# Sixteen broadcast loads of a state-space scan issued by GpSimd instead of SyncE

## The chip, the core and the metric

The kernel runs on one core of one Trainium2 chip. The metric is the device time of one execution in microseconds (us); lower is better. Three executions of the kernel before took 815.21, 816.28 and 816.71 us, so its median is 816.28 us. A core has five instruction streams that run side by side and wait for each other through semaphores: PE (TensorE, matrix products; PEld is its weight load), DVE (VectorE), ACT (ScalarE), POOL (GpSimd) and SP (SyncE, which here issues DMAs and does nothing else). Each stream takes its instructions strictly in order. Sixteen DMA engines move the data of every DMA, whichever stream issued it.

## The reference

The program is one decoder block on 16 meta tokens and 512 real ones: an input projection, a Mamba-2 mixer (SSD) and an S5 mixer side by side, an output projection and an MLP. The part that the change touches is the inside of the SSD mixer. Cut to that part:

```python
a_cs = jnp.cumsum(dtc * a, axis=2)
seg = a_cs[:, :, :, None] - a_cs[:, :, None, :]
decay = jnp.exp(jnp.where(causal, seg, -jnp.inf))
cb = jnp.einsum('bclgn,bcsgn->bclsg', cc, bc)
y_diag = jnp.einsum('bclsg,bclsgr,bcsgrp->bclgrp', cb, decay, xdt)
y_off = jnp.einsum('bclgn,bcgrpn,bclgr->bclgrp', cc, prev, jnp.exp(a_cs))
y = (y_diag + y_off + xc * d)
```

`a_cs` is one running sum for each of 16 heads along the tokens. The kernel needs it, and its exponential, spread over partitions: a row of 128 tokens of one head has to stand in all 128 partitions (`decay`), and a row of `exp(a_cs)` in the 64 partitions of its head (`y_off`).

## The kernel before

The work goes by stages that overlap. First come the input projection's columns for S5 (`u`), for the SSD inputs (`pxb`) and for the gate (`pz`), with the eight blocks of the S5 scan (`s5_block`) between them; then the S5 mixer's gated projection with `w_glu` (`pv`, `pg`, line 891 on); then the output projection with `w_out` (`acc`) and the MLP in four quarters. Nearly every matrix product is done three times, because float32 operands are split into a high and a low part: ACT writes `whi`, and DVE (`wlo`, line 118) or an adding DMA from POOL (line 122) writes the low part. The weights come in through three buffers of one kind (`raw`, line 105): SP loads 512 KB into one, in 1024 rows of 512 bytes for `w_in` and `w_glu`, and can load into it again when the low part of the weights that stood there has been written.

The SSD scan is the loop over `ch` at line 735. It runs over the 16 meta tokens (chunk 0) and four chunks of 128 tokens, with a state `S` of 16 heads that each chunk updates. It is placed by a scheduler between the matrix products of the gated projection, which runs at the same time. The scheduler sets the order of each engine's instructions when the program is built, so an engine meets both kinds of work in one fixed order.

For each of chunks 1 to 4:

- `erep` (line 766) gets `exp(a_cs)`: two loads, each to 64 partitions, of 8 rows of 512 bytes per partition. That is 256 KB and 512 rows in one load. There is one buffer, so the load waits until DVE has multiplied with the chunk before (`yt`, line 796).
- `ab` (line 771) gets `a_cs`, for 8 heads at a time: two loads, for `g` = 0 and 1, each to 128 partitions of 8 rows of 512 bytes. That is 512 KB and 1024 rows in one load. There are two buffers, so each load waits until the products of the chunk before that used this buffer (`pyd`, line 789) are done.
- POOL then puts the causal mask on `ab` (`affine_select`, line 773), ACT takes the exponential of the 8 heads (line 777), DVE multiplies it by `cb` (line 779), and PE uses it as the moving operand of `pyd`.
- PE also makes `pyo` from the state (line 793), DVE adds the parts up (lines 796 to 803), ACT squares the result (line 805), DVE adds the squares up in `sqs`, and PE sums those over the partitions into `pq1` (line 813).

`aD` and `eD`, which hold `a_cs` and its exponential in DRAM, were written long before (lines 671 and 672).

The S5 blocks before this stage have a chain of small DMAs of their own: a block's `lag` goes to DRAM (`Kd`, line 539), comes back shifted in four loads as `Tp` (line 541), and is the weight of the block's `py` products (line 594). Block 7 is the last one.

Of the kernel before, what the change touches and what calls it, by code (L numbers as in the profile page):

```python
# [18 lines left out]
P = 128  # L19
# [26 lines left out]
def bc(ap, axis, n):  # L46
    a = ap.unsqueeze(axis)
    shape = list(a.shape)
    shape[axis] = n
    return a.broadcast_to(shape)  # L50
# [3 lines left out]
def hybrid_block_kernel(ctx, tc, x, meta_tokens, g_mix, w_in, conv_w, conv_b, dt_bias, a_log, d_ssd,  # L54
                        g_ssd, lam_re, lam_im, log_step, b_re, b_im, c_re, c_im, d_s5, w_glu, b_glu,
                        g_s5, w_out, g_mlp, w_up, w_down, g_final, out, dbg=None):
    nc = tc.nc
    V, A, G, T = nc.vector, nc.scalar, nc.gpsimd, nc.tensor
    dma = nc.sync.dma_start
    dma2 = nc.sync.dma_start  # L60
# [18 lines left out]
    def bank(name, dt=F32):  # L79
        tag = KIND.get(name, "x")  # L80
        return ps.tile([P, 512], dt, tag=tag, name=name, bufs=TAGS[tag])
# [16 lines left out]
    def vadd(out, in0, in1):  # L98
        V.tensor_tensor(out=out, in0=in0, in1=in1, op=ALU.add)  # L99
# [367 lines left out]
    def col(nm, i):  # L467
        c = row[nm] + i
        return pcol[:, c:c + 1]
# [199 lines left out]
    aD = dr.tile([NH, SEQ], F32, name="aD")  # L669
# [61 lines left out]
    erep = sd.tile([P, KD, P], F32, tag="erep", name="erep", bufs=1)  # L731
# [3 lines left out]
    for ch in range(NCH):  # L735
        n = NM if ch == 0 else P
        t0 = 0 if ch == 0 else NM + (ch - 1) * P
        tk = slice(t0, t0 + n)

        pcb = bank("pcb")  # L740
        if ch > 0:
            for g in range(2):
                T.matmul(pcb[:, g * P:(g + 1) * P], lhsT=bcT[:, g, tk], rhs=bcT[:, 2 + g, tk])
        if ch < 4:
            btok = sd.tile([P, 2, P], F32, tag="btok", name="btok", bufs=1)
            for g in range(2, 4):
                T.transpose(pcb[0:n, g * P:(g + 1) * P], bcT[:, g - 2, tk], ident)
            A.copy(btok[0:n], pcb[0:n, 2 * P:4 * P].rearrange("p (g q) -> p g q", g=2))
        if ch > 0:
            xdt = sd.tile([P, NH, 64], F32, tag="xdt", name="xdt", bufs=1)  # L750
            xde = sd.tile([P, NH, 64], F32, tag="xde", name="xde", bufs=1)
        for h in range(2):
            ptx = bank("ptx")
            for k in range(4):
                T.transpose(ptx[0:n, k * P:(k + 1) * P], xc[:, 4 * h + k, tk], ident)
            pv = ptx[0:n].rearrange("p (h d) -> p h d", d=64)
            hs = slice(8 * h, 8 * h + 8)
            if ch > 0:
                V.tensor_tensor(out=xdt[0:n, hs], in0=pv, in1=bc(dt[0:n, ch, hs], 2, 64), op=ALU.mult)
            if ch < 4:  # L760
                V.tensor_tensor(out=xde[0:n, hs], in0=pv, in1=bc(wdt[0:n, ch, hs], 2, 64), op=ALU.mult)
        if ch > 0:
            lt = slice((ch - 1) * P, ch * P)
            if ch > 1:
                erep = sd.tile([P, KD, P], F32, tag="erep", name="erep", bufs=1)
            for q in range(2):
                dma2(out=erep[64 * q:64 * q + 64],
                     in_=eD.rearrange("(r q) l -> q r l", q=2)[q, :, lt].partition_broadcast(64))
            Gm = []
            for g in range(2):  # L770
                ab = sd.tile([P, 8, P], F32, tag="ab", name="ab", bufs=2)
                dma2(out=ab, in_=aD[8 * g:8 * g + 8, lt].partition_broadcast(P))
                G.affine_select(out=ab, in_=ab, pattern=[[0, 8], [1, P]], compare_op=ALU.is_ge, fill=-1e30, base=0,
                                channel_multiplier=-1)
                with tc.issue_after(last_silu.ins):
                    for h in range(8):
                        A.activation(out=ab[:, h], in_=ab[:, h], func=AF.Exp,
                                     bias=neg_a[:, ch, 8 * g + h:8 * g + h + 1])
                V.tensor_tensor(out=ab, in0=ab, in1=bc(pcb[:, g * P:(g + 1) * P], 1, 8), op=ALU.mult)
                Gm.append(ab)  # L780
            for h in range(2):
                pyd = bank("pyd")
                pyo = bank("pyo")
                for r in range(4):
                    pr = 4 * h + r
                    o = slice(r * P, (r + 1) * P)
                    for q in range(2):
                        hd = 2 * pr + q
                        T.matmul(pyd[64 * q:64 * q + 64, o], lhsT=xdt[:, hd], rhs=Gm[h][:, hd % 8])
                for r in range(4):  # L790
                    pr = 4 * h + r
                    o = slice(r * P, (r + 1) * P)
                    T.matmul(pyo[:, o], lhsT=S[0][:, 2 * pr:2 * pr + 2].rearrange("p a b -> p (a b)"),
                             rhs=bcT[:, 2 + h, tk])
                yt = sd.tile([P, 4, P], F32, tag="yt", name="yt")
                V.tensor_tensor(out=yt, in0=pyo.rearrange("p (r l) -> p r l", r=4), in1=erep[:, 4 * h:4 * h + 4],
                                op=ALU.mult)
                V.tensor_tensor(out=yt, in0=yt, in1=pyd.rearrange("p (r l) -> p r l", r=4), op=ALU.add)
                for r in range(4):
                    pr = 4 * h + r  # L800
                    V.scalar_tensor_tensor(out=yt[:, r], in0=xc[:, pr, tk], scalar=col("D", pr), in1=yt[:, r],
                                           op0=ALU.mult, op1=ALU.add)
                V.tensor_tensor(out=xc[:, 4 * h:4 * h + 4, tk], in0=yt, in1=sz[:, 4 * h:4 * h + 4, lt], op=ALU.mult)
                sq = sd.tile([P, 4, P], F32, tag="sq", name="sq", bufs=1)
                A.activation(out=sq, in_=xc[:, 4 * h:4 * h + 4, tk], func=AF.Square)
                vadd(sq[:, 0:2], sq[:, 0:2], sq[:, 2:4])
                if h == 0:
                    sqs = sd.tile([P, P], F32, tag="sqs", name="sqs", bufs=1)
                    vadd(sqs, sq[:, 0], sq[:, 1])
                else:  # L810
                    vadd(sq[:, 0], sq[:, 0], sq[:, 1])
                    vadd(sqs, sqs, sq[:, 0])
                    T.matmul(pq1[:, ch - 1:ch], lhsT=sqs, rhs=ones[:, 0:1])
        if ch < 4:
            for g in range(2):
                pst = bank("pst")
                T.matmul(pst, lhsT=btok[0:n, g], rhs=xde[0:n, 8 * g:8 * g + 8].rearrange("p a b -> p (a b)"))
                sv = S[0][:, 8 * g:8 * g + 8]
                pv = pst.rearrange("p (a b) -> p a b", b=64)
                if ch == 0:  # L820
                    V.tensor_copy(sv, pv)
                else:
                    V.tensor_tensor(out=sv, in0=sv, in1=bc(cdec[:, ch, 8 * g:8 * g + 8], 2, 64), op=ALU.mult)
                    V.tensor_tensor(out=sv, in0=sv, in1=pv, op=ALU.add)
# [640 lines left out]
```

## Time and profile before

| | before |
|---|---|
| median of three runs | 816.28 us |
| the profiled execution: its own time | 814.91 us |
| the profiled execution: span of its instructions | 813.2 us |
| DVE busy, share of the span | 77% |
| ACT busy | 61% |
| POOL busy | 10% |
| mean traffic of all DMAs | 150 GB/s |

The profile is one execution, recorded by the hardware. Times in its rows are in us from the start of the span. A row of its timeline gives start, length, engine, line of the kernel, operation, what is written and read, how many equal instructions in a row, and in brackets the idle time of the engine before it with what ended it. "q" behind an engine's name (SPq) is its sequencer, where DMAs are issued: the length of such a row is that of the issuing, not of the transfer. The view of stretches gives the busy time of each engine, the granted clock of PE (1.00 is full speed) and the busy share of the DMA engines.

The scan's chunks 1 to 4 use PE from 288 to 359 us of the span, in the middle of the gated projection.

### The profile page before, as it was taken

The numbers are of one execution on the slowest core, as the hardware profiler recorded it, in microseconds if no ns is written. First come the engines' busy times: TensorE is split into PE (matmuls) and PEld (weight loads), VectorE is DVE, ScalarE is ACT, GpSimd is POOL, SyncE is SP. The second block draws the span as 40 slices with busy tenths as digits, with TensorE's granted clock in tenths as the row PEclk, the third lists the DMA queues.
The fourth block names the chain that finished last, engine by engine and source line by source line (L and its number), as shares of the span: only waits on it lengthen the run. The fifth ranks groups of instructions, "written<-read, shape, count | busy, mean of one in ns | idle before, by whom it ended". The sixth has DMA issues, their size and how long they took to land. (4 is left out here: it accounts for less than half of the span.)

```text
span 813.2 us, 12926 instructions
## 1 busy us (share of the span) xinstructions
PE 772.9 (95%) x4943; PEld 682.4 (84%) x4943; DVE 625.9 (77%) x972; ACT 495.7 (61%) x782; POOL 78.6 (10%) x125
## 2 busy tenths in 40 slices
PE   6999899989999998999999998989999999999996
PEld 6999898988787776788888887868997899789975
DVE  4479798989776579897434588698779877987897
ACT  7568799888654565456213476654665477546665
POOL 3201000011000111000000000100010001000101
PEclk9999999999999999999999999999999999999999
DMA  8998675766764645345235118865495548654622
GB/s 238 180 219 202 155 164 137 182 142 160 164 159 130 177 123 140 108 126 197 88 104 160 48 52 261 192 156 164 134 182 155 157 134 179 181 162 114 115 52 104
DMA packets 129638, 121.90 MB, mean 150 GB/s; under 512 B 21836, under 2 KB 105720, under 8 KB 129576
## 3 DMA queue, kind: packets, MB, share of 16 engines
q1 hardware_dynamic: 121224, 90.66, 38.3%
q0 software_dynamic: 8352, 30.41, 20.4%
q8 instruction: 39, 0.64, 0.3%
q14 instruction: 23, 0.19, 0.1%
HBM read 83.76 MB, written 6.88 MB: 111 GB/s over the span
## 5 line engine op out<-in xcount | busy, mean ns | idle before, releaser
L1018 DVE TENSOR_TENSOR wlo<-quad,whi 128x1024 fp32r<-128x1024 f32 x40 | 48.9, 1223 | 35.2 <-ACT whi L1017 35.0
L1017 ACT CAST whi<-quad 128x1024 fp32r<-128x1024 f32 x40 | 41.9, 1048 | 53.4 <-DMA quad<-raw 17.7
L1240 PE MATMUL u<-opC,whi 128*128 128x256 f32 x384 | 70.1, 285 | 2.3 <-DVE r L99 1.1
L1281 PE MATMUL acc<-whi,al 128*128 128x512 f32 x160 | 63.4, 396 | 3.5 <-DVE al L1018 3.5
L1240 PEld LDWEIGHTS u<-opC,whi 128*128 128x128 f32 x384 | 59.5, 191 | 3.4 <-DVE r L99 1.6
L1281 PE MATMUL acc<-whi,ah 128*128 128x512 f32 x160 | 59.6, 393 | 2.7 <-ACT ah L1017 2.7
L1281 PE MATMUL acc<-wlo,ah 128*128 128x512 f32 x160 | 60.4, 390 | 0.0
L118 DVE TENSOR_TENSOR wlo<-raw,whi 128x1024 fp32r<-128x1024 f32 x31 | 37.9, 1221 | 29.0 <-ACT whi L117 28.6
L117 ACT CAST whi<-raw 128x1024 fp32r<-128x1024 f32 x31 | 32.4, 1044 | 42.7 <-PE acc L840 32.6
L139 PE MATMUL pxb<-xhi,whi 128*128 128x264 f32 x192 | 55.3, 288 | 1.6 <-ACT xcr L695 1.6
L139 PE MATMUL pxb<-xhi,wlo 128*128 128x264 f32 x192 | 55.9, 291 | 0.0
L139 PE MATMUL pxb<-xlo,whi 128*128 128x264 f32 x192 | 55.7, 290 | 0.0
L1017 ACT CAST whi<-bquad 128x1024 fp32r<-128x1024 f32 x34 | 35.7, 1049 | 29.2 <-PE acc L1281 19.6
L1240 PE MATMUL u<-opC,wlo 128*128 128x256 f32 x192 | 53.2, 283 | 0.0
L1240 PE MATMUL u<-opB,whi 128*128 128x256 f32 x256 | 48.5, 289 | 1.2 <-DVE opB L1018 0.7
L1240 PE MATMUL u<-opA,whi 128*128 128x256 f32 x256 | 45.9, 280 | 0.3 <-ACT whi L1017 0.3
L1018 DVE TENSOR_TENSOR wlo<-bquad,whi 128x1024 fp32r<-128x1024 f32 x34 | 41.5, 1220 | 3.2 <-ACT whi L1017 3.2
L1240 PEld LDWEIGHTS u<-opB,whi 128*128 128x128 f32 x256 | 40.9, 196 | 1.6 <-DVE opB L1018 0.9
L1281 PEld LDWEIGHTS acc<-whi,al 128*128 128x128 f32 x160 | 30.1, 188 | 13.2 <-DVE al L1018 7.3
L1240 PEld LDWEIGHTS u<-opA,whi 128*128 128x128 f32 x256 | 39.2, 188 | 0.8 <-ACT whi L1017 0.5
L122 POOL DMA_DIRECT2D wlo<-raw x26 | 22.3, 856 | 181.4 <-ACT xcr L695 53.3
L123 ACT CAST whi<-raw 128x1024 fp32r<-128x1024 f32 x26 | 27.1, 1043 | 18.4 <-PE pu L139 7.5
(435 smaller groups left out, 2447.7 us busy)
## 6 DMA issues: line engine op xcount, KB each, us to landing
raw<-in_w_in_dram SPq DMA_DIRECT2D x28, 512.0 KB, 4.2
wlo<-raw POOLq DMA_DIRECT2D x26, 512.0 KB, 5.4
raw<-in_w_up_dram SPq DMA_DIRECT2D x22, 512.0 KB, 4.8
raw<-in_w_glu_dram SPq DMA_DIRECT2D x16, 512.0 KB, 4.5
raw<-in_w_out_dram SPq DMA_DIRECT2D x16, 512.0 KB, 3.6
bquad<-in_w_down_dram SPq DMA_DIRECT2D x16, 512.0 KB, 3.8
quads<-in_w_down_dram SPq DMA_DIRECT2D x16, 512.0 KB, 4.3
bquad<-quads POOLq DMA_DIRECT2D x16, 512.0 KB, 5.3
```

What stands on the lines that cost most here:

```text
L117: A.copy(hi, raw)
L118: V.tensor_tensor(out=lo, in0=raw, in1=hi.bitcast(F32), op=ALU.subtract)
L122: G.dma_start(out=lo.bitcast(F32), in_=raw, accum_op=ALU.add)
L123: A.copy(hi, raw)
L139: T.matmul(ps_out, lhsT=w[a][:, k, 0:m], rhs=x[b][:, k, tok], start=(n == 0), stop=(n == len(steps) - 1))
L1017: A.copy(hi, src)
L1018: last_low[:] = [V.tensor_tensor(out=lo, in0=src, in1=hi.bitcast(F32), op=ALU.subtract)]
L1240: T.matmul(pb[:, mm], lhsT=w[a][:, k, mm * P:(mm + 1) * P], rhs=x[:, b, k], start=(first and n == 0), stop=(n in (11, 23)), skip_group_che ...
L1281: T.matmul(banks[s], lhsT=at[x][:, g, j, s * P:(s + 1) * P], rhs=wt[y][:, j], start=(fresh and g == 0 and j == 0 and k == 0), stop=(g == 1 ...
```

## The change

The two `dma2` calls of the loop become `G.dma_start`. `dma2` is SP's, `G` is GpSimd. The 8 loads of `erep` and the 8 of `ab` are issued by POOL, into the same buffers, with the same sizes. Nothing else in the source is changed.

```diff
             for q in range(2):
-                dma2(out=erep[64 * q:64 * q + 64],
+                G.dma_start(out=erep[64 * q:64 * q + 64],
                      in_=eD.rearrange("(r q) l -> q r l", q=2)[q, :, lt].partition_broadcast(64))
             Gm = []
             for g in range(2):
                 ab = sd.tile([P, 8, P], F32, tag="ab", name="ab", bufs=2)
-                dma2(out=ab, in_=aD[8 * g:8 * g + 8, lt].partition_broadcast(P))
+                G.dma_start(out=ab, in_=aD[8 * g:8 * g + 8, lt].partition_broadcast(P))
                 G.affine_select(out=ab, in_=ab, pattern=[[0, 8], [1, P]], compare_op=ALU.is_ge, fill=-1e30, base=0,
                                 channel_multiplier=-1)
```

The scheduler places the instructions anew. On POOL, in the stretch of the scan, there were eight masks in a row behind the last adding DMA of the projection (`wlo<-raw`); before:

```order
L122 DMA wlo<-raw 128x1024 x23
L773 AFFINE_SELECT ab<-ab 128x1024 x8
L829 TENSOR_TENSOR ssd_s<-ssdq,mhalf 128x4
```

And the same place now:

```order
L122 DMA wlo<-raw 128x1024 x23
L767 DMA erep<-eD 64x8x128 x2
L772 DMA ab<-aD 128x8x128 x2
L773 AFFINE_SELECT ab<-ab 128x1024 x2
L772 DMA ab<-aD 128x8x128 x2
L773 AFFINE_SELECT ab<-ab 128x1024
L767 DMA erep<-eD 64x8x128 x2
L773 AFFINE_SELECT ab<-ab 128x1024
L772 DMA ab<-aD 128x8x128 x2
L767 DMA erep<-eD 64x8x128 x2
L773 AFFINE_SELECT ab<-ab 128x1024 x2
```

The first four loads stand behind the last adding DMA of the projection. Of what they wait for, the last to be done is ACT's copy of block 7's `decay` (line 578). In chunk 2 the second mask stands behind the two loads of `erep`, in chunk 3 both masks do, and in chunk 4 again the second one (it follows below these rows).

On SP, the piece of the difference in the same stretch: the loads of the scan leave the queue, and ten loads of `w_glu` that stood between them follow each other.

```order
 L708 DMA yf<-Yd_1008 128x512
 L708 DMA yf<-Yd_1009 128x512
-L767 DMA erep<-eD 64x8x128 x2
-L772 DMA ab<-aD 128x8x128 x2
-L106 DMA raw<-in_w_glu_dram 128x8x128 x4
-L772 DMA ab<-aD 128x8x128 x2
-L767 DMA erep<-eD 64x8x128 x2
-L106 DMA raw<-in_w_glu_dram 128x8x128 x2
```

Each of these ten still waits for its `raw` buffer; what is gone is the waits of the scan's loads ahead of them.

On PE, the piece of the difference at chunk 2, where `pyd`, `pyo` and `pq` stand among the products of the gated projection (`pg`):

```order
 L139 MATMUL pg<-yglo,whi 128x512
+L139 MATMUL pg<-yghi,wlo 128x512
 L789 MATMUL pyd<-ab,xdt 64x128 x8
 L793 MATMUL pyo<-bcr,S 128x128 x4
 L789 MATMUL pyd<-ab,xdt 64x128 x8
-L793 MATMUL pyo<-bcr,S 128x128 x2
+L793 MATMUL pyo<-bcr,S 128x128 x4
 L813 MATMUL pq_3130<-ones,sqs 128x1
-L793 MATMUL pyo<-bcr,S 128x128 x2
-L139 MATMUL pg<-yghi,wlo 128x512
```

One more product of the projection now stands ahead of chunk 2, and all four `pyo` of its second half stand ahead of `pq`. In chunk 3 the scan's products stand six of the projection's later than before, in chunk 4 twelve.

## The prediction

> **What bounds the kernel now.** I read the page's busy times first, then the stretches of 10 us around the scan, then PE's own timeline.
>
> ```profile
> PE 772.9 (95%) x4943; PEld 682.4 (84%) x4943; DVE 625.9 (77%) x972; ACT 495.7 (61%) x782; POOL 78.6 (10%) x125
> 240.00:250.00 10.00, 9.45 (x57) 8.17 (x56) 8.05 (x15) 4.82 (x5) 0.00 (x0) 1.00 0.38 94
> ...
> 270.00:280.00 10.00, 10.00 (x46) 6.82 (x44) 8.03 (x11) 5.38 (x6) 1.01 (x1) 1.00 0.70 156
> 280.00:290.00 10.00, 10.00 (x60) 8.05 (x58) 5.66 (x7) 8.29 (x22) 2.18 (x2) 1.00 0.48 142
> ...
> 300.00:310.00 10.00, 9.49 (x58) 7.53 (x57) 7.41 (x14) 9.16 (x23) 1.59 (x2) 1.00 0.45 101
> 310.00:320.00 10.00, 8.16 (x47) 6.60 (x48) 9.97 (x20) 3.26 (x9) 1.46 (x1) 0.83 0.77 206
> ```
>
> The columns behind the length are PE, PEld, DVE, ACT and POOL busy, the granted clock, the DMA share and GB/s. PE is the bound: 95% of the whole, and full or nearly so in each stretch. So a load that comes earlier gains only where PE stands still for want of it, and one that comes later costs as soon as PE meets it. PE's idle times (in brackets) between block 7's `py` and the end of the scan that matter are these four:
>
> ```profile
> 243.78 0.46 PE L594 MATMUL py<-ub,Tp 128*128 128x128 f32 x2 [0.56 <-DVE tw L573]
> 308.83 1.09 PE L789 MATMUL pyd<-ab,xdt 128*64 128x128 f32 x16 [0.51 <-DVE xdt L759]
> 314.59 0.38 PE L813 MATMUL pq<-ones,sqs 128*128 128x1 f32 x2 [1.78 <-DVE sqs L99]
> 356.94 0.38 PE L813 MATMUL pq<-ones,sqs 128*128 128x1 f32 x2 [0.33 <-DVE sqs L99]
> ```
>
> An idle time has a second price, the granted clock:
>
> ```profile
> 165.31 1.08 PE L528 MATMUL pk<-CC,WB 128*32 128x128 f32 x16 [2.43 <-ACT btr L521]
> 166.00:170.00 4.00, 4.00 (x30) 3.68 (x23) 3.98 (x7) 2.35 (x7) 0.00 (x0) 0.68 0.69 131
> 207.75 0.46 PE L594 MATMUL py<-ub,Tp 128*128 128x128 f32 x2 [1.66 <-DMA Tp<-Kd]
> 206.00:210.00 4.00, 2.34 (x12) 1.93 (x12) 3.92 (x9) 0.80 (x2) 0.00 (x0) 1.00 0.42 99
> 312.00:316.00 4.00, 2.22 (x16) 1.84 (x13) 3.97 (x8) 1.24 (x2) 0.00 (x0) 0.91 0.79 227
> 316.00:320.00 4.00, 4.00 (x13) 3.09 (x12) 4.00 (x10) 2.02 (x7) 1.46 (x1) 0.66 0.91 238
> ```
>
> After 2.43 and 1.78 us of idling the clock falls to 0.68 and 0.66 for 4 us; after 1.66 it stays at 1.00. In chunk 2 that cost (1 - 0.66) x 4 + (1 - 0.91) x 4 = 1.7 us. So all that the scan loses is 0.51 + 1.78 + 1.7 + 0.33 = 4.3 us: **the most the change can gain**.
>
> **What is removed.** On SP the loads stood between weight loads that wait for their buffer:
>
> ```profile
> 238.50 0.39 SPq L106 DMA_DIRECT2D raw<-in_w_glu_dram  x1
> 239.65 1.74 SPq L541 DMA_DIRECT2D Tp<-Kd  x4
> 266.44 1.36 SPq L767 DMA_DIRECT2D erep<-eD  x2
> 267.84 4.03 SPq L772 DMA_DIRECT2D ab<-aD  x2
> 290.57 1.67 SPq L772 DMA_DIRECT2D ab<-aD  x2
> ```
>
> Chunk 1's four loads left at 266.4 to 271.9, though their data and buffers were there from 234.5 on. Nothing is gained by that in chunk 1, since PE is busy for all of the 18 us ahead of its first `pyd` at 288 (270 to 290 above). In the later chunks SP was prompt: chunk 2's loads left at 290.57, and PE had finished with the first buffer at 289.1:
>
> ```profile
> 288.00 1.09 PE L789 MATMUL pyd<-ab,xdt 128*64 128x128 f32 x16
> 333.74 1.09 PE L789 MATMUL pyd<-ab,xdt 128*64 128x128 f32 x16
> ```
>
> SP is rid of 16 issues of about 0.6 us; PE waited for no weights there, so I cost that at nothing, bounded by the 4.3 above.
>
> **What is added: POOL's time for an issue.** The only DMAs that POOL issues in the trace are adding ones, of 512 KB in 128 rows of 4 KB:
>
> ```profile
> L122 POOL DMA_DIRECT2D wlo<-raw x26: 841/854/1023, 13.3 to 226.8; - x26
> ```
>
> No row shows POOL issuing 1024 rows (`ab`) or 512 (`erep`). Were the 0.85 us a price per issue, both would take 0.85; were it a price per row, 8 x 0.85 = 6.8 and 4 x 0.85 = 3.4. SP's issues show no price per row (0.39 for the 1024 rows of `raw` above, 1.74 for four loads `Tp` of at most 128), but SP is another path. I take an estimate between the two ends by ratio, sqrt(0.85 x 6.8) = 2.4 for `ab` and sqrt(0.85 x 3.4) = 1.7 for `erep`, and keep both ends. The Trainium skill, "DMA: Bandwidth & Descriptors", section on the anatomy of a DMA on the gpsimd path, calls descriptor generation small: one can emit many before the added cost shows. By that rule the lower ends hold and the sum below would be +1.3 in place of +2.2; no run here shows it yet.
>
> **Step 1, the burst of chunk 1.** POOL's loads start behind this copy, at 234.5:
>
> ```profile
> 233.91 0.63 ACT L578 COPY decay<-mag 128x524 f32<-128x524 f32 x1 [0.81 <-DVE wi L581]
> q1 hardware_dynamic: 121224, 90.66, 38.3%
> ```
>
> A row of SP's queue costs 0.383 x 16 x 813.2 / 121224 = 41 ns of one engine. The four loads have 2 x 512 + 2 x 1024 = 3072 rows, 192 for each of 16 engines, or 7.9 us; issued 1.7 + 1.7 + 2.4 + 2.4 = 8.2 us long, they keep the engines busy from about 236 to 244. In that time block 7's `Tp` loads go out (239.65), behind a 512 KB `raw` (238.50): 1024 + 512 rows, 3.9 us of engine time, at half speed while both queues have work. That brings `Tp` some 2 us later, and the `py` at 243.78, which already came after an idle 0.56, needs it (in the block before, `Tp` ended an idle 1.66, above). I take **+1.9** of idling, and since 0.56 + 1.9 = 2.5 is above the idle times after which the clock fell, **+1.7** for the clock: +3.6, bounds 0 and 4.5. The skill's page says in "Issuing engines are not separate DMA queues" that such DMAs share the 16 engines and interleave, and that another issuer saves issuing time alone: this rule speaks against the change, and with it the +3.6 stays.
>
> **Step 2, chunks 2 to 4: POOL in order.** The masks now stand behind POOL's own issues:
>
> ```profile
> 297.60 2.42 POOL L773 TENSOR_SCALAR_AFFINE_SELECT ab<-ab 128x1024 f32<-128x1024 f32 x1 [14.94 <-DMA ab<-aD]
> 300.69 1.58 POOL L773 TENSOR_SCALAR_AFFINE_SELECT ab<-ab 128x1024 f32<-128x1024 f32 x1 [0.67 <-DMA ab<-aD]
> 316.48 1.46 POOL L773 TENSOR_SCALAR_AFFINE_SELECT ab<-ab 128x1024 f32<-128x1024 f32 x1 [14.22 <-DVE yt L796]
> 321.04 1.21 POOL L773 TENSOR_SCALAR_AFFINE_SELECT ab<-ab 128x1024 f32<-128x1024 f32 x1 [3.10 <-DVE xcr L803]
> 347.15 1.37 POOL L773 TENSOR_SCALAR_AFFINE_SELECT ab<-ab 128x1024 f32<-128x1024 f32 x1 [5.19 <-PE ptx L755]
> 296.05 0.68 DVE L796 TENSOR_TENSOR yt<-pyo,erep 128x512 f32<-128x512 f32 x1
> 317.51 0.68 DVE L796 TENSOR_TENSOR yt<-pyo,erep 128x512 f32<-128x512 f32 x1
> 300.05 3.63 ACT L777 ACTIVATE ab<-ab,neg_a 128x128 f32<-128x128 f32 x12 [5.85 <-POOL ab L773]
> 329.49 2.33 DVE L779 TENSOR_TENSOR ab<-ab,pcb 128x1024 f32<-128x1024 f32 x2
> ```
>
> Chunk 2: the two issues take 289.1 to 293.9; the first landing comes 297.60 - 290.57 = 7.0 after its issue, at about 297; mask 1 to 298.4 (1.4 long), `erep` (its `yt` ends at 296.7) 3.4 to 301.8, mask 2 to 303.2, 0.9 later than now (302.27). But mask 1 ends 1.6 earlier, and ACT's square, which stood behind 12 exponentials, stands behind 8. So DVE's chain is about 1 us earlier, the 0.51 goes, and the 1.78 before `pq` shrinks a little, to about 1.6 (one DVE step of 0.6 now stands ahead), which by the rows above leaves the clock at 1.00: -0.5 - 0.2 - 1.7 = **-2.4**.
>
> Chunk 3: both masks wait behind `erep`, whose `yt` ends at 318.2: issues to 321.6, masks to 323.0 and 324.4, against 317.94 and 322.25. ACT's 16 exponentials (4.9 us) end near 327.9, before the 329.49 at which DVE multiplied; but ACT's other work behind them comes 2.7 later and DVE waits for part of it. PE's new order gives 1.4 (six products) of cover: **+1.0**, bounds 0 and 2.7.
>
> Chunk 4: the second `ab` no longer queues behind weight loads; mask 2 ends some 2 us earlier than the 348.5 of now, and PE comes to it later by order: the 0.33 may go, no more. I take **0**.
>
> **Sum:** +3.6 - 2.4 + 1.0 = +2.2. The profiled execution took 814.91, which gives 817.1; it lies 1.37 below the median of 816.28, so the median after comes to **818.5 us**, slower by 0.27%. A measurement of this kernel can tell about 0.2% (1.6 us) from no change.
>
> **Rivals.** *POOL becomes the bound.* At 6.8 and 3.4 per issue, chunk 2's second mask ends at 289.1 + 13.6 + 1.4 + 6.8 + 1.4 = 312.3, 10 us later than now; in chunks 3 and 4 the same 23.2 us stand between the end of the first `pyd` and the second mask, against 12.3 (309.9 to 322.25) and 13.7 (334.8 to 348.5): 10.9 and 9.5 later. Less about 1 + 3 + 1 of cover that makes +25, and +1 from a thinner burst: 842. It decides from the point where the two issues outlast the landing, 2 x issue > 7.0, so from 3.5 us per `ab`; there it costs some +5, at 4.5 some +13. For it: 8 times the rows; against it: nothing in the trace, and the skill's rule.
>
> *Faster.* The burst doesn't reach `Tp` in time to hurt, or PE was held there by DVE's `tw`, which the profile names, and `Tp` has slack: step 1 is 0. If chunk 3's delay is hidden too, the sum is -2.4, or 813.9; with all four idle times and the clock's fall gone it is -4.3, or 812.0.
>
> *No change.* Issues are cheap (0.85): `erep` in chunk 3 is 1.7 sooner and its +1.0 falls to 0.1, so +1.3; or both price and gain are hidden: 814.7 to 817.9. The skill's rule above gives this one.
>
> **Chances.** Forecast (817.9 to 822) 0.34; POOL as bound (822 to 842) 0.20; faster 0.22; no change 0.24. So faster 0.22, same 0.25 (a little of the forecast's edge lies there), slower 0.53. The range of 8 in 10 goes from 812.5 to 833; it leaves out the best of the faster case and the upper half of POOL as bound. The likeliest case alone spans 816 to 822.
>
> **What would show it.** In the profile after: POOL's rows of `ab<-aD` and `erep<-eD` at 2.4 and 1.7 us (0.85: no change; 6.8: POOL is the bound); PE's idle time before the first `py` with `Tp` at 2.5 in place of 0.56, and a clock below 1.00 in the 4 us behind it; no idle time before chunk 2's `pyd`, less than 1.7 before its `pq`, and a clock of 1.00 there; POOL's masks of chunk 2 near 297 and 302 less what PE is shifted. The forecast is wrong if `Tp` lands in time, or if an `ab` issue takes more than 3.5 us.

## The result and the profile after

The changed kernel takes **823.68 us** (median of 6, 822.01 to 825.91); the kernel before took 815.90 us in the same series (median of 6, 815.14 to 817.71). The ratio is 1.0102, 95% interval 1.0086 to 1.0118: slower by 1.0%, 7.8 us. The profiled execution after took 825.91 us (span 824.2), 11.0 more than the one before; 3.2 of these 11.0 are scatter of the two executions. The ratios here and below are of the normal executions of a series and not the quotients of the medians shown; a few executions of the later series were far slower (948 to 3359 us) and are left out of the ratios.

The page after: engines, and POOL's DMA queue (q0) with packets, MB and share of the engines' time. The last line is the same queue on the page of before.

```profile
PE 773.6 (94%) x4943; PEld 682.8 (83%) x4943; DVE 626.8 (76%) x972; ACT 495.5 (60%) x782; POOL 88.7 (11%) x141
q0 software_dynamic: 10144, 36.70, 24.4%
q0 software_dynamic: 8352, 30.41, 20.4%
```

PE's work is what it was (773.6 against 772.9 us) and POOL has 10 us more of its own: no engine became the bound. PE lost the time by waiting. To find where, I took landmarks in PE's order and read their times in both timelines: the first `pv` behind block 7's `py` and the first product of the output projection (L840; a row gives shortest/median/longest ns, then first and last start), before and after in turn.

```profile
253.64 0.50 PE L139 MATMUL pv<-yghi,whi 128*128 128x512 f32 x1 [0.28 <-ACT sz L701]
264.79 0.51 PE L139 MATMUL pv<-yghi,whi 128*128 128x512 f32 x1 [0.29 <-ACT sz L701]
L840 PE MATMUL acc<-whi,y5hi x64: 387/389/486, 381.8 to 425.6; 128*128 128x512 f32 x64
L840 PE MATMUL acc<-whi,y5hi x64: 387/389/481, 388.7 to 432.6; 128*128 128x512 f32 x64
```

| stretch | before | after | difference |
|---|---|---|---|
| start to that `pv` | 253.64 | 264.79 | +11.15 |
| from there to the first L840 | 128.2 | 123.9 | -4.2 |
| from there to the end of the span | 431.4 | 435.5 | +4.1 |

So three things happened. **The loss is one place.** These are PE's timeline and the stretches behind it in the changed kernel (columns: length, busy PE, PEld, DVE, ACT, POOL, granted clock, DMA share, GB/s):

```profile
252.91 0.77 PE L594 MATMUL py<-ub,Tp 128*128 128x128 f32 x2 [9.85 <-DMA Tp<-Kd]
246.00:250.00 4.00, 0.00 (x0) 0.00 (x0) 2.31 (x3) 0.00 (x0) 1.56 (x2) 0.64 0.73 189
250.00:254.00 4.00, 1.08 (x4) 1.02 (x5) 0.00 (x0) 0.00 (x0) 0.72 (x1) 0.50 0.40 97
254.00:258.00 4.00, 4.00 (x12) 3.12 (x11) 1.07 (x1) 2.13 (x2) 0.00 (x0) 0.58 0.06 15
258.00:262.00 4.00, 4.00 (x19) 3.22 (x18) 3.45 (x5) 0.79 (x2) 0.00 (x0) 1.00 0.45 131
```

Block 7's `py` waits 9.85 us for `Tp` where it had waited 0.56: 9.3 us. The clock has fallen meanwhile, and the first work behind the gap runs at about half speed (12 products in 254 to 258, 19 in the 4 us behind): the other 1.9 of the 11.15. The sequencers of POOL and SP in the changed kernel, and in the last line `Kd` in the kernel before:

```profile
234.68 1.47 POOL L767 DMA_DIRECT2D erep<-eD  x2 [7.21 <-ACT decay L578]
236.12 1.82 POOL L772 DMA_DIRECT2D ab<-aD  x2
237.90 0.34 SPq L539 DMA_DIRECT2D Kd<-lag  x1
238.34 1.89 SPq L106 DMA_DIRECT2D raw<-in_w_glu_dram  x1
249.78 1.74 SPq L541 DMA_DIRECT2D Tp<-Kd  x4
...
238.06 0.34 SPq L539 DMA_DIRECT2D Kd<-lag  x1
```

POOL issues chunk 1's four loads in 3.3 us. `Kd` goes out at 237.90 as before (238.06), but `Tp`, which waits until `Kd` has landed, is issued at 249.78 instead of 239.65. So not the `Tp` loads are late in moving: the 64 KB store ahead of them is. The queues from 237 to 243, changed kernel first, then the kernel before:

```profile
q0 software_dynamic: 249, 0.86, 86.3%
q1 hardware_dynamic: 1760, 0.75, 48.1%
```

After the change SP's queue does not appear in these 6 us at all: `Kd` and a weight load were issued, and not one of their packets began. POOL's queue moved 0.86 MB in 249 packets, 3.5 KB on average, where SP's rows had gone as packets of 512 bytes. By the packets of the trace, SP's last one before ran at 236.7 and its next at 243.3; the burst ran from 236.2 to 248.9, 12.7 us long.

**The gain is there too:** of chunk 2's idle times of 0.51 and 1.78 us and its slow clock nothing is left (its products now stand in the stretch below, in which PE is full and the clock is 1.00), and the stretch to L840 is 4.2 us shorter.

```profile
320.00:324.00 4.00, 4.00 (x50) 3.54 (x48) 4.00 (x8) 1.24 (x2) 1.34 (x2) 1.00 0.74 183
```

**Behind L840** 4.1 us come back, most of it scatter, but not all; that is taken up below.

### The profile page after: what moved, and what is told of

The parts are those of the page before. It is cut to its first block, busy times and chain, and to the rows that moved or that the text cites. A ratio compares the mean times of both kernels' runs of the same rounds, so it can differ in the third digit from the quotient of the medians.

```text
span 824.2 us, 12919 instructions
## 1 busy us (share of the span) xinstructions
PE 773.6 (94%) x4943; PEld 682.8 (83%) x4943; DVE 626.8 (76%) x972; ACT 495.5 (60%) x782; POOL 88.7 (11%) x141
## 3 DMA queue, kind: packets, MB, share of 16 engines
q0 software_dynamic: 10144, 36.70, 24.4%
## 5 line engine op out<-in xcount | busy, mean ns | idle before, releaser
L1240 PE MATMUL u<-opC,whi 128*128 128x256 f32 x384 | 71.9, 289 | 6.8 <-ACT whi L1017 5.1
```

Of the source, the lines that this page charges most:

```text
L1240: T.matmul(pb[:, mm], lhsT=w[a][:, k, mm * P:(mm + 1) * P], rhs=x[:, b, k], start=(first and n == 0), stop=(n in (11, 23)), skip_group_che ...
```

## The experiments

The theory after these views: the loss is the collision of chunk 1's burst (1.5 MB) with the store of `Kd`, nothing else, and it goes when the burst stands elsewhere. The rivals: POOL's queue harms SP's wherever it stands; the size of POOL's packets does it; any 1.5 MB at this moment would do it; another transfer than `Tp` is the victim. Medians (of 4 to 12 executions, where it doesn't say once) are beside those of the kernel before in the same series.

### Chunk 1's loads back on SP, or only these on POOL

```diff
-                G.dma_start(out=erep[64 * q:64 * q + 64],
+                (dma2 if ch == 1 else G.dma_start)(out=erep[64 * q:64 * q + 64],
...
-                G.dma_start(out=ab, in_=...)
+                (dma2 if ch == 1 else G.dma_start)(out=ab, in_=...)
```

> Chunk 1's four loads go back to SyncE, those of chunks 2 to 4 stay on GpSimd. Theory (the loss is the collision of chunk 1's burst with the store of Kd and the loads of Tp, nothing else): the idle time before that py falls from 9.85 us to about 0.6, the clock there stays 1.00, and the gain at chunk 2 (the gaps of 0.51 and 1.78 us and the slow clock behind them, about 4.2 us) stays: 815.9 - 4.2, about 811.7 us, 810.5 to 813. Rival (the later chunks' loads cost too, beside the weights): about 815.9 or more.

Measured: 813.53 us against 815.93, ratio 0.9972 (0.9956 to 0.9988): the loss turns into a gain. Its `py`, chunk 2's `pq`, and the stretches around the latter:

```profile
244.48 0.46 PE L594 MATMUL py<-ub,Tp 128*128 128x128 f32 x2 [0.95 <-DVE wi L575]
314.98 0.38 PE L813 MATMUL pq<-ones,sqs 128*128 128x1 f32 x2 [1.41 <-DVE sqs L99]
312.00:316.00 4.00, 2.59 (x23) 2.10 (x20) 4.00 (x8) 1.24 (x2) 0.89 (x1) 1.00 0.97 250
316.00:320.00 4.00, 4.00 (x17) 2.93 (x16) 4.00 (x8) 0.00 (x0) 1.71 (x3) 1.00 0.76 171
```

`py` is in time. The gain is 2.4 us, not 4.2: chunk 2's `pq` still waits 1.41 us, short enough for the clock to stay at 1.00. In chunk 3, too, 0.44 and 0.24 us of waiting are new. My sum had taken the whole gain from the changed kernel, where PE came to chunk 2 some 11 us later.

The other half has the same edit with G and `dma2` exchanged.

> Only chunk 1's four loads on GpSimd, the twelve others back on SyncE. Theory: the loss alone, 9.3 us of idle time before py and about 1.8 us of slow clock behind it, without the gain at chunk 2: 815.9 + 11, about 827 us, 825 to 829. Rival (the loss and the gain at chunk 2 hang together, because the shift of 11 us itself gives the weights time to arrive and removes the gap there): about 823, with no gap before chunk 2's pyd and pq even so.

Measured: 827.02 us against 815.93, ratio 1.0132 (1.0095 to 1.0168), with these two waits:

```profile
254.38 0.76 PE L594 MATMUL py<-ub,Tp 128*128 128x128 f32 x2 [9.14 <-DMA Tp<-Kd]
349.67 0.38 PE L813 MATMUL pq<-ones,sqs 128*128 128x1 f32 x2 [1.74 <-DVE sqs L99]
```

So +11.1 alone and -2.4 for the rest; together +8.7, measured together +7.8. The two parts add up within 1 us. The rival had a point: chunk 2's gap is gone here too, but 1.74 us of waiting stand before chunk 3's `pq` in its place.

### The same loads on POOL, later

```diff
+    hold, held = mid.tile([P, 4], F32, tag="hold", name="hold", bufs=1), []
...
-        A.activation(out=yb, in_=py..., func=AF.Gelu)
+        A.activation(out=yb, in_=py..., func=AF.Gelu); b == 7 and held.append(G.tensor_copy(out=hold, in_=yb[:, 0, 0:4]))
...
+                with tc.issue_after(held[0].ins) if ch == 1 else nullcontext(): G.dma_start(...)
```

> All 16 loads on GpSimd, but chunk 1's four wait there behind a copy of 4 numbers of the last block's yb, so that they start after its py instead of 10 us before it. Theory (the moment, not the queue, makes the loss): the same as with chunk 1 on SyncE, about 811.7 us, 810.5 to 813.5; the idle time before py about 0.6 us. Rival (a software queue hurts the hardware queue wherever it stands): a new idle time of over 1.5 us before the next products or the yf loads, and 815 or more.

Measured: 827.04 us, ratio 1.0131 (1.0111 to 1.0151): **the theory missed by 15 us** (2 of them belong to the new tile, as the next kernels show). `py` is in time now (0.60), and PE waits at another place; with the queues in 262 to 272:

```profile
269.43 0.80 PE L139 MATMUL pv<-yghi,whi 128*128 128x512 f32 x1 [5.15 <-ACT yghi L709]
274.44 0.79 PE L139 MATMUL pv<-yghi,whi 128*128 128x512 f32 x1 [2.50 <-ACT yghi L709]
q0 software_dynamic: 376, 1.32, 72.4%
q1 hardware_dynamic: 531, 0.64, 20.6%
```

The burst left at 258.9, and block 7's `Yd` stores and the `yf` loads that bring them back (SP, from 258.6) were beside it: the next trip through DRAM on which PE waits. I had looked only at `Tp`. This is also what the rival had forecast, so this kernel alone does not decide between a bad moment and a queue that does harm wherever it stands; the next one does. It waits for the last `yf` instead (`f == 7 and held.append(G.tensor_copy(out=hold, in_=yf[:, 0:4]))`).

> All 16 loads on GpSimd, chunk 1's four behind a copy of 4 numbers of the last yf, so behind the last of the transfers through DRAM (near 267, where SyncE issues them when they are its own). Theory (a burst on GpSimd's queue stops what SyncE has under way, and costs only where TensorE waits for that: the last block's Tp near 240, the yf loads near 260, only weights with a reserve behind 267): no idle time over 1 us between 240 and 330, and about the time of the run with chunk 1 on SyncE, 812.5 to 815. Rival (GpSimd's queue costs with every burst): an idle time of over 2 us between 267 and 300, and 817 or more.

Measured: 816.19 us against 816.75, ratio 1.0006 (0.9987 to 1.0024). No wait over 0.6 us is left between 240 and 330, as the theory wanted: the moment matters, and there are two moments to keep off. Yet 2 us are missing. They are in L840, which the edit doesn't touch; from its first to its last product it is 91.7 us here and 89.6 before. The row of this kernel, to be read beside that of before (389 ns, above):

```profile
L840 PE MATMUL acc<-whi,y5hi x64: 392/396/481, 375.5 to 420.5; 128*128 128x512 f32 x64
```

312 of the 384 products of this line take 395 to 396 ns, the other 72 are as before. The new tile of 16 bytes a partition displaces all tiles behind it. In the last of the series it has 512 bytes, with the same instructions:

```diff
-    hold, held = mid.tile([P, 4], F32, tag="hold", name="hold", bufs=1), []
+    hold, held = mid.tile([P, P], F32, tag="hold", name="hold", bufs=1)[:, 0:4], []
```

> As the run with chunk 1's loads held back behind the last yf, but the little tile for the copied numbers takes 512 B of a partition instead of 16, so that the tiles behind it keep their distance from a multiple of 512. In the held-back run the 384 products of L840 took 396 ns instead of 389-390, 2.1 us in all, with the same instructions. Theory (the 16 B displaced their operands): 390 ns again, and 816.2 - 2.1 = 814.1 us, 812.5 to 815.5. Rival (the products slow down for another reason, such as the traffic): 396 ns and about 816.

Measured: 814.55 us against 816.55, ratio 0.9971 (0.9956 to 0.9985).

```profile
L840 PE MATMUL acc<-whi,y5hi x64: 387/389/481, 377.9 to 421.8; 128*128 128x512 f32 x64
```

The products are back at 389 ns, `py` waits 0.45 us, and the time came out 0.45 us from what was expected. All 16 loads on POOL are as good as twelve, if chunk 1's leave behind the trips through DRAM.

### Is `Tp` the victim?

Block 7 builds `Tp` with 16 ACT copies, as block 0 does, without a trip through DRAM; the burst stays where it was:

```diff
-        if b == 0:
+        if b in (0, 7):
...
-        for t in range(TS5 if b else 0):
+        for t in range(TS5 if b not in (0, 7) else 0):
```

> All 16 loads on GpSimd at the same moment as in the changed kernel, but the last block builds Tp by 16 ScalarE copies from pk as the first block does, so that it has no store of Kd and no loads of Tp. Theory (the store and the loads of Tp are the burst's only victims that matter): the burst looks the same and the idle time before py is under 1 us although the DMA share in 238-250 stays above 0.7; 16 x 0.216 = 3.5 us more on ScalarE fit into its idle 4.4 us; about 811.7 us, 810.5 to 813.5. Rival (the late weight of in_w_glu or another transfer behind the burst stops TensorE as well): an idle time of over 3 us in 243 to 260 remains and the time is 815 or more.

Measured: 817.71 us against 815.93, ratio 1.0014 (0.9995 to 1.0033): not 1.0102, though the burst is as dense as there. The queues from 239 to 245 (POOL's is the only one), then PE's two waits in `py`, and the two DVE instructions that made them late:

```profile
q0 software_dynamic: 241, 0.84, 80.0%
254.42 0.49 PE L595 MATMUL py<-sr,CC 128*128 128x128 f32 x2 [1.52 <-DVE sr L587]
256.91 0.80 PE L597 MATMUL py<-si,CC 128*128 128x128 f32 x2 [1.30 <-DVE si L590]
248.27 1.60 DVE L589 TENSOR_TENSOR si<-wr,sni 128x528 f32<-128x528 f32 x1
252.21 1.41 DVE L585 TENSOR_TENSOR tw<-wi,sni 128x528 f32<-128x528 f32 x1
```

No wait for a transfer is left before `py`. 2.8 us for DVE have come in its place. The 16 copies are not to blame: they end at 242.9, and the first `py` with `Tp` at 244.46 does not wait. The two DVE instructions shown took 0.70 and 0.71 us in the kernel before; each stands here beside one of chunk 1's masks on POOL (247.78 and 251.23), which come this early because the loads do. That the masks slow them is likely, but no run separates it. So the trip of `Kd` and `Tp` was the victim; this is no cure.

### What in the burst does it?

Here the 16 loads are back on SP, and three loads of 512 KB more go from `aD` to a DRAM buffer that nobody reads (so they write DRAM and not SBUF), at the moment of `Kd`'s store; once issued by POOL, once by ACT (`nc.scalar`, with `A.copy`, and with the wide `hold`):

```diff
-            dma2(out=Kd[b], in_=lag)
+            hv = G.tensor_copy(out=hold, in_=lag[:, 0:4]) if b == 7 else None; dma2(out=Kd[b], in_=lag)
...
+        with tc.issue_after(hv.ins) if b == 7 else nullcontext(): [G.dma_start(out=spare[k], in_=aD[0:8, 0:P].partition_broadcast(P)) for k in range(3 if b == 7 else 0)]
```

> The kernel before, with three loads of 512 KB more, issued by GpSimd as soon as the last block's lag is there (a copy of 4 numbers of it goes ahead), from aD into a buffer that nobody reads: the same source pattern and 1.5 MB as chunk 1's burst, at the moment of the store of Kd, with the 16 loads themselves on SyncE as before. Theory (traffic on GpSimd's queue at this moment is enough, the loads themselves and their later readers have no part): the idle time before py is 5 us or more and the time 822 to 830. Rival (it needs the loads of ab and erep, through the tiles or their release): under 2 us of idle time, 815 to 818. Its twin with the same three loads on ScalarE's queue is to follow and tells the queue from the bytes.

> The twin of the run with the three foreign loads on GpSimd: the same three loads of 512 KB at the same moment behind lag, but issued by ScalarE, so on the hardware queues. Theory (it is GpSimd's queue that holds the engines): the store of Kd and the loads of Tp take turns with the burst, the idle time before py is under 4 us, where the twin had 8.07. Rival (1.5 MB ahead of or beside them cost this on any queue): 7 to 12 us. ScalarE's own issue time, if long, delays its yb and shows as another wait.

Measured once each: 827.32 and 821.69 us (before: 816.75 and 816.55). First POOL's run, then ACT's, `py` and the queues from 240 to 246 (q10 is ACT's):

```profile
254.61 0.77 PE L594 MATMUL py<-ub,Tp 128*128 128x128 f32 x2 [8.07 <-DMA raw<-in_w_glu_dram]
q0 software_dynamic: 170, 0.63, 88.0%
q1 hardware_dynamic: 252, 0.12, 8.8%
```

```profile
254.13 0.77 PE L594 MATMUL py<-ub,Tp 128*128 128x128 f32 x2 [6.16 <-DMA Yd<-yb]
q10 hardware_dynamic: 1216, 0.61, 52.7%
q1 hardware_dynamic: 1022, 0.51, 40.0%
```

With POOL the idle time is what the theory said; ACT's 6.16 lies above its 4 and below the rival's 7, nearer to the rival. Both idle times are less than the delay: in these two kernels the scheduler has put products of `pz` between block 7's `px` and its `py`, 23 (5.4 us) with POOL and 28 (6.5 us) with ACT, where there are none before. From `Kd`'s issue to this `py` it is 18.6 us with POOL, 17.8 with ACT, 15.0 in the changed kernel and 5.7 before. `Kd` itself landed after 1.6 us in both; what came late are the loads of `Tp`, of which one took 14.9 us with POOL and one 13.0 with ACT (the releasers in the brackets are other DMAs that landed then). So, by these two runs, **most of the loss comes from 1.5 MB at this moment, on whichever queue**: it costs 5.1 us on ACT's queue and 10.6 on POOL's, of which 2 are the 16-byte tile that only POOL's run still had. With POOL's queue PE idles 1.9 us longer there, and 0.8 us longer passes from `Kd` to `py`, as far as one execution each can tell; the rest of the difference was not followed up. The change is dear less because it is POOL that issues than because POOL, with an empty queue, issues 32 us before SP did.

The queues show how the engines are shared. Between ACT and SP it goes packet by packet (1216 to 1022), and between POOL and SP also (170 to 252), but a packet of POOL's has 8 times the bytes. The Trainium skill, "DMA: Bandwidth & Descriptors", section "Queues, rings and completion order", says that each DMA engine takes the queues in turn, a packet at a time; these two runs agree. The changed kernel does not (249 to none). What differs is who was first. In POOL's run with foreign loads, SP had a weight load and `Tp` under way when the burst's first packet ran at 239.2; in the changed kernel the first packet ran at 236.2, SP's queue ran dry at 236.7, and `Kd` left at 237.90. In the run with the burst at 258.9, `Yd` had left first, and SP's queue had its turns (531 to 376). The time for which the queue that comes second gets nothing grows with the burst: from the burst's first packet to SP's next one it is 7.1 us in the changed kernel and 7.3, 7.9 and 7.3 in three others with all of chunk 1's loads at this moment (chunk 1 alone on POOL, `Tp` by copies, and the wider rows below), but 2.5 with `erep`'s third of it (below). Why is not shown by any run.

To make POOL's packets small, the tiles got rows of 136 numbers (`sd.tile([P, 8, P + 8], ...)[:, :, 0:P]`, `erep` alike), so that the destination is not in one piece:

> As the changed kernel, but the tiles ab and erep have rows of 136 numbers of which 128 are used, so that no two source rows of 512 B land side by side. If GpSimd's queue builds its 4096 B packets because the destination is in one piece, it now has 8 times as many of 512 B. Theory A (the hardware queue gets no turn, or one per packet at most, because each packet holds a DMA engine for 328 ns): with packets of some 41 ns the store of Kd lands within 2 us and the idle time before py falls from 9.85 us to under 3; about 815. Theory B (an engine works off what GpSimd's queue has handed it first, whatever its packets): the idle time stays 8 to 11 us and the time 822 to 828, and GpSimd's issues, with 8 times the descriptors, stay under 1.5 us or the skill's flat price is wrong.

Measured: 825.41 us against 816.75, ratio 1.0110 (1.0089 to 1.0131).

```profile
251.87 0.77 PE L594 MATMUL py<-ub,Tp 128*128 128x128 f32 x2 [8.89 <-DMA Tp<-Kd]
q0 software_dynamic: 258, 0.90, 85.1%
```

The packets (237 to 243) are as long as before, 3.5 KB on average, so **this run does not tell the theories apart**: POOL's queue packs 8 rows of 512 bytes together with this destination too. The changed kernel's page has it too: 10144 - 8352 = 1792 packets more, 16 small ones for each of 16 loads and 1536 for 12,288 rows. The Trainium skill, "DMA: Bandwidth & Descriptors", section "SWDGE vs HWDGE vs iDMA", gives 4096 bytes as the preferred limit of a packet on this path; the trace agrees.

### Half of the burst

Of chunk 1's loads, only those of `ab`, or only those of `erep`, stay on POOL:

> As the changed kernel, but of chunk 1's loads only the two of ab (1.0 MB) are on GpSimd, the two of erep on SyncE. Theory (Kd waits until the burst is over): the 384 packets took 236.2 to 248.7, 12.5 us, so 256 take 8.3 us, to about 244.6; in the changed kernel py began 4.2 us after the burst's end, so here near 248.8, an idle time of 5.8 us, 4 to 7.5. Rival (the length is set by something else, such as the late weight): 9 to 10 us as in the changed kernel, or under 1.

> The other half: of chunk 1's loads only the two of erep (0.5 MB) on GpSimd, the two of ab on SyncE. Theory: 128 packets take 4.2 us, to about 240.4, py near 244.6, an idle time of 1.6 us, 0.5 to 2.5. Rival as there: 9 to 10 us, or no difference from the kernel before (0.56).

Measured once each: 818.36 and 815.02 us (before: 816.55). With `ab` alone, POOL's sequencer and the longest wait; then `erep` alone:

```profile
227.03 2.19 POOL L772 DMA_DIRECT2D ab<-aD  x2
239.95 1.22 PE L570 MATMUL px<-ub,btr 128*128 128x132 f32 x4 [4.51 <-issue]
245.15 0.46 PE L594 MATMUL py<-ub,Tp 128*128 128x128 f32 x2 [2.48 <-DMA Tp<-Kd]
```

`erep` fits: 2.48, at the upper edge of what was expected. Its burst came first too (from 236.0 to 240.5, `Kd` left at 237.50), and `Tp`, which waits for `Kd` to land, left at 241.95, 4.4 us behind it. `ab` was a miss: its buffers come free earlier than `erep`'s, behind whose loads it had stood in POOL's order. So the burst left at 227.0, and the wait is before an S5 block's `px`: the last of the `ub` loads for it, issued by SP at 233.1, moved its rows of 528 bytes from 236.5 to 239.5. It tells nothing on the length. As far as one execution can tell, it shows again that the victim is whatever PE needs next through SP's queue.

### Only chunk 2's loads on POOL

G where `ch == 2` and `dma2` elsewhere, to take the gain alone:

> Only chunk 2's four loads on GpSimd. Theory: the idle times of 0.51 and 1.78 us before chunk 2's pyd and pq and the slow clock behind them go, 815.9 - 4.2 = 811.7 us at best; if the 2 us by which the run with twelve loads missed its sum go with the number of loads on GpSimd's queue, this one comes out nearer to it than 813.5. Rival (the gain is worth no more than 2.4 us wherever it is taken, since the gap returns later): 813 to 815.9.

Measured: 817.00 us against 816.75, ratio 1.0007 (0.9991 to 1.0024). Chunk 2's waits shrink to 0.38, but new ones come in chunk 3:

```profile
334.76 1.09 PE L789 MATMUL pyd<-ab,xdt 128*64 128x128 f32 x16 [1.89 <-DVE ab L779]
339.06 0.39 PE L813 MATMUL pq<-ones,sqs 128*128 128x1 f32 x2 [1.54 <-DVE sqs L99]
```

So the gain is taken and given back a chunk later. That is the rival's reason, though the time lies outside its range as well. The gain stayed in the runs above, in which chunks 3 and 4 move too.

## Why the prediction was right, and where it was not

Slower was right, and for the reason given: chunk 1's loads leave some 32 us earlier, into block 7's trip through DRAM, and its `py` waits for `Tp` while the clock falls. The size was not: 7.8 us instead of 2.2. The time lies inside the range by luck: 823.68 is beyond the 817.9 to 822 of the forecast itself and among the times given for POOL as the bound (822 to 842), which did not happen.

- **The bound.** "The most the change can gain" was 4.3 us; the stretch with these four waits became 4.2 us shorter. Held.
- **POOL's price for an issue.** Taken as 2.4 and 1.7, between 0.85 and 6.8 or 3.4. Measured:

```profile
L772 POOL DMA_DIRECT2D ab<-aD x8: 882/911/933, 236.1 to 345.9; - x8
L767 POOL DMA_DIRECT2D erep<-eD x8: 687/694/757, 234.7 to 354.6; - x8
```

  It is a price per issue, near the low end; twice the rows cost 0.22 us more. The rule of the Trainium skill that the prediction quotes ("DMA: Bandwidth & Descriptors", section on the anatomy of a DMA on the gpsimd path) held. The +1.3 that the prediction had worked out for this price is further from 7.8 than its +2.2. POOL as the bound, at 0.20 the heaviest rival for the range, was never near: it needed 3.5.
- **Step 1**, +3.6, is **the step that failed in size**: 9.3 us of idling and 1.9 of clock, 11.2 in all, and the run with chunk 1 alone on POOL confirms it (+11.1). The wrong step is "at half speed while both queues have work". I let the `Tp` loads share the engines with the burst and counted on `Kd`, ahead of them, landing as before (1.6 us after its issue). But `Kd` itself was caught, and it got not half of the engines, but none from 237 to 243. The burst was mis-sized as well: 12.7 us of packets, not 7.9. Even the upper bound of 4.5 was too low, since it allowed nothing worse than sharing. That DMAs of different issuers interleave, as the Trainium skill has it (same page, "Issuing engines are not separate DMA queues"), held in the two runs with foreign loads and not in the changed kernel.
- **Step 2, chunk 2**, -2.4. With chunk 1 out of the way it is about what was worked out: the first wait gone, the second shortened (to 1.41; forecast 1.6), the clock at 1.00, and 2.4 us gained in the median. In the changed kernel, where PE is 11 us late, all 4.2 are gained.
- **Step 2, chunk 3**, +1.0: not seen in the changed kernel; no wait of 0.2 us or more stands there (0.44 and 0.24 with chunk 1 on SP). It rested on the dear issue, and at 0.9 the masks are early enough. **Chunk 4**, 0: held (0.33 to 0.31).
- **Not foreseen: the MLP.** No instruction changes there, yet in all six kernels with all 16 loads on POOL PE waits 2.6 to 2.8 us at one place, against 0.9 to 1.2 in the eight others, the kernel before among them. Before and after, the first adding DMA there, SP's weight loads beside it, and the wait:

```profile
487.01 0.90 POOL L1012 DMA_DIRECT2D quad<-raw  x1 [12.80 <-issue]
487.66 5.44 SPq L1057 DMA_DIRECT2D raw<-in_w_up_dram  x2
493.85 0.39 PE L1240 MATMUL u<-opC,whi 128*128 128x256 f32 x1 [1.04 <-ACT whi L1017]
...
494.46 0.97 POOL L1012 DMA_DIRECT2D quad<-raw  x1 [13.28 <-issue]
494.62 7.17 SPq L1057 DMA_DIRECT2D raw<-in_w_up_dram  x2
502.54 0.61 PE L1240 MATMUL u<-opC,whi 128*128 128x256 f32 x3 [2.76 <-ACT whi L1017]
```

  Before, POOL issues 0.65 us ahead of SP; after, 0.16. By the packets POOL's come first before (488.5 against 489.2) and SP's come first after (495.7 against 497.8), and the adding DMA then lands 6.9 instead of 5.7 us after its issue. These 1.2 us and POOL's 0.5 make the 1.7 that PE waits longer, a contest for the engines again, in small. Why POOL is half a microsecond later there stays open, and no run was made on it.

In sum, 11.2 for block 7, -4.2 for the scan and 1.7 in the MLP make 8.7, by one profiled execution each, of 7.8 measured between the medians. The forecast's own errors ran against each other only in part: step 1 was 7.6 too small, step 2 (-1.4 in all) 2.8 too high.

## What to carry to other kernels

An engine with an empty queue issues a load as soon as its buffer is free, which can be tens of microseconds before anyone wants it (SP issued these 32 us later and PE did not wait for them in chunk 1): before giving loads to such an engine, look at what the DMA engines have to deliver at that new moment, above all short trips through DRAM on which the busiest engine waits. If something stands there, hold the load behind it (814.55 and 813.53 us instead of 823.68). And a transfer that meets a burst on the engines is not bounded by half speed; reckon with the burst's whole length (`Kd` took 11.9 us beside a burst of 12.7).

## What the runs showed of the hardware

- A store of 64 KB on SP's queue that lands 1.6 us after its issue took nearly 12 behind a burst of 1.5 MB on POOL's queue, with no packet in the first 5 us. A store issued 0.2 us ahead of such loads kept its 1.6, as their first packet came only 3 us later. With a third of the burst ahead of it, the store took 4.4 us at most.
- POOL's queue makes packets of 4096 bytes out of rows of 512, SP's queue leaves them at 512; where the two take turns by packets, SP's gets 0.12 MB while POOL's gets 0.63.
- 16 bytes more in front of the tiles make 312 products with a moving operand of 128x512 slower, 396 ns instead of 389, with no change to these instructions, and with 512 bytes they are back at 389: 2 us of the whole.
